# Binary cross-entropy on one core: from a software DMA queue with casting loads to one hardware queue with float32 half loads

## The chip, the core and the metric

The kernel runs on one core of a Trainium2 chip. The metric is the device time of one execution in microseconds (us). Engines: DVE is VectorE, ACT is ScalarE, POOL is GpSimd, SP is SyncE (SPq is SP's own queue of instructions). The 16 DMA engines that carry the transfers are a different thing from these engines, and they are what this study is about.

## The reference

```python
# pred, target: (8192, 8192) float32, target is 0 or 1
pred = np.clip(pred, 1e-7, 1 - 1e-7)
return -(target * np.log(pred) + (1 - target) * np.log(1 - pred))
```

Because target is 0 or 1, this equals -ln|target - 1 + clip(pred)|. Two tensors of 268 MB are read and one of 268 MB is written, with four cheap passes between.

## The kernel before

The tensors are taken as flat arrays and cut into chunks: 4096, 4096, 8192 columns, then thirty chunks of 16384, then 8192, 4096, 2048, 1024, 1024 (columns per partition, 128 partitions). A chunk is contiguous in memory, so each of the 128 partitions gets one run; in a full chunk that is 64 KiB of float32. `ring_p` holds two full chunks of pred, computed in place and stored from there. `ring_t` holds two full chunks of target in bfloat16: POOL's software queue casts while it loads.

```python
RING = 32768
SUB = 2048
ring_p = pool.tile([P, RING], fp32, ...)
ring_t = pool.tile([P, RING], bf16, ...)

def load(k):
    c, w = at(k), widths[k]
    nc.gpsimd.dma_start(out=ring_t[:, c : c + w], in_=dram(target_f, cols[k], w))
    nc.gpsimd.dma_start(out=ring_p[:, c : c + w], in_=dram(pred_f, cols[k], w))

def front(c, w):        # two DVE and two ACT instructions
    ...
def back(c, w):         # DVE: times -1
    ...
def compute(k):
    c, w = at(k), widths[k]
    n = max(1, w // SUB)
    s = w // n
    for i in range(n):
        front(c + i * s, s)
        if i:
            back(c + (i - 1) * s, s)
    back(c + (n - 1) * s, s)
```

A chunk's loads are issued as soon as the stores that free its place in `ring_p` have been issued; the pred load then waits until that store has landed, that is, until all 16 DMA engines have reported it complete.

## Time and profile before

| | |
|---|---|
| time, median of 3 runs | 1870.94 us |
| span of the profiled run | 1868.8 us |
| DVE busy, ACT busy | 63%, 52% |
| software DMA queue, share of 16 engines | 99.9% |
| HBM traffic | 805.3 MB, 431 GB/s |

These are lines of the page of the kernel before: the DMA's busy tenths, its packets, the queues with their packets, MB and share of the 16 engines' span, and the traffic.

```profile
DMA  9999999999999999999999999999999999999998
DMA packets 16427, 671.19 MB, mean 359 GB/s; under 512 B 1824, under 2 KB 1824, under 8 KB 2720
q0 software_dynamic: 16416, 671.10, 99.9%
q14 instruction: 11, 0.09, 0.0%
HBM read 536.87 MB, written 268.44 MB: 431 GB/s over the span
```

The DMA is busy all the time. 671 MB are moved as counted at the destination, because a cast target arrives as half its bytes; 805 MB is what HBM sees.

From the chain of waits (start us, length us, what), the pieces in which nothing but the transfers was waited for, every second chunk:

```profile
474.93 36.09 issue
...
591.20 36.14 issue
...
707.42 36.21 issue
```

Two chunks take 116.2 us, 58.1 us each. Now the end, by the windows view: stretch and length in us, busy us of DVE, ACT and POOL, clock, DMA share, GB/s moved.

```profile
1818.00:1832.00 14.00, 11.15 (x9) 10.27 (x6) 0.32 (x1) 1.00 1.09 435
1832.00:1845.00 13.00, 9.93 (x8) 7.53 (x4) 1.60 (x2) 1.00 0.96 416
1845.00:1853.00 8.00, 4.05 (x4) 3.82 (x2) 0.36 (x1) 1.00 0.97 420
1853.00:1858.00 5.00, 2.75 (x4) 2.11 (x2) 0.70 (x2) 1.00 0.89 378
1858.00:1861.00 3.00, 0.97 (x1) 1.97 (x2) 0.00 (x0) 1.00 0.59 242
1861.00:1863.00 2.00, 0.69 (x1) 0.15 (x1) 0.00 (x0) 1.00 0.13 55
1863.00:1865.00 2.00, 0.00 (x0) 0.00 (x0) 0.25 (x1) 1.00 0.05 20
1865.00:1867.00 2.00, 0.00 (x0) 0.00 (x0) 0.29 (x1) 1.00 0.59 242
```

The rate falls from 435 GB/s to 20 and rises once more for the last store. The timeline of the same end (start, length, engine, what, idle before it and its releaser) shows the last two instructions:

```profile
1861.18 0.69 DVE L94 TENSOR_SCALAR ring_p<-ring_p 128x1024 f32<-128x1024 f32 x1 [2.21 <-ACT ring_p L90]
1864.75 0.54 POOL L79 DMA_DIRECT2D out_dram<-ring_p  x1 [6.82 <-issue]
```

The last DVE instruction ends at 1861.87, and the last store goes out 2.9 us later: POOL hesitates once. The trace doesn't say why.

### The profile page before, as it was taken

How to read it: one execution, taken by the hardware profiler on the slowest of the kernel's cores; microseconds unless marked ns; L12 is line 12 of the kernel's file. 1: busy time of each engine (PE TensorE's matmuls, PEld its weight loads, DVE VectorE, ACT ScalarE, POOL GpSimd, SP SyncE). 2: the span in 40 equal slices, each digit the busy share in tenths (PEclk: the TensorE clock that was granted, in tenths of full speed). 3: DMA queues.
4: the chain of work that ended last, by engine and by line, in shares of the span. 5: the costliest groups of instructions: out<-in, count | busy, mean ns of one | idle time of the engine just before them, and what ended most of it. 6: DMA issues, size and time to landing. Idle time of an engine off the chain costs nothing.

```text
span 1868.8 us, 1563 instructions
## 1 busy us (share of the span) xinstructions
DVE 1178.6 (63%) x772; ACT 976.3 (52%) x516; POOL 65.4 (3%) x118
## 2 busy tenths in 40 slices
DVE  4557755577555775557755577555776556755595
ACT  3446544565444654446544466444664446644474
POOL 1000000000000000000000000000000000000010
DMA  9999999999999999999999999999999999999998
GB/s 292 359 358 338 348 400 371 337 355 342 393 386 339 341 352 387 384 351 339 345 386 389 351 344 337 383 395 344 352 344 365 400 358 339 354 355 395 374 335 349
DMA packets 16427, 671.19 MB, mean 359 GB/s; under 512 B 1824, under 2 KB 1824, under 8 KB 2720
## 3 DMA queue, kind: packets, MB, share of 16 engines
q0 software_dynamic: 16416, 671.10, 99.9%
q14 instruction: 11, 0.09, 0.0%
HBM read 536.87 MB, written 268.44 MB: 431 GB/s over the span
## 4 chain that ended last, share of the span: by engine, by line
DMA 34%; issue 30%; DVE 27%; ACT 7%; POOL 1%; another core or an unknown queue 1%; POOLq 0%; PEldq 0%
DMA ring_p<-in_pred_dram 32%; DVE ring_p L86 13%; DVE ring_p L94 7%; DVE ring_p L83 7%; ACT ring_p L89 3%; ACT ring_p L90 3%; DMA out_dram<-ring_p 2%; POOL out_dram L79 1%; POOL ring_t L74 1%; POOL ring_p L75 0%; POOLq L151 0%; POOLq L79 0%; PEldq L151 0%
## 5 line engine op out<-in xcount | busy, mean ns | idle before, releaser
L89 ACT ACTIVATE ring_p<-ring_p 128x2048 f32<-128x2048 f32 (+1 forms) x257 | 488.9, 1902 | 876.0 <-DVE ring_p L86 876.0
L83 DVE TENSOR_SCALAR ring_p<-ring_p 128x2048 f32<-128x2048 f32 (+1 forms) x257 | 312.9, 1218 | 552.9 <-DMA ring_p<-in_pred_dram 552.9
L86 DVE SCALAR_TENSOR_TENSOR ring_p<-ring_t,ring_p 128x2048 f32<-128x2048 bf16 (+1 forms) x257 | 586.9, 2284 | 8.8
L90 ACT ACTIVATE ring_p<-ring_p 128x2048 f32<-128x2048 f32 (+1 forms) x257 | 489.2, 1903 | 8.1
L94 DVE TENSOR_SCALAR ring_p<-ring_p 128x2048 f32<-128x2048 f32 (+1 forms) x257 | 313.1, 1218 | 120.8 <-ACT ring_p L90 120.8
L75 POOL DMA_DIRECT2D ring_p<-in_pred_dram x38 | 21.9, 576 | 1094.1 <-DMA out_dram<-ring_p 1084.9
L79 POOL DMA_DIRECT2D out_dram<-ring_p x38 | 22.1, 581 | 700.3 <-DVE ring_p L94 689.9
L74 POOL DMA_DIRECT2D ring_t<-in_target_dram x38 | 21.8, 574 | 5.3 <-DMA ring_t<-in_target_dram 4.4
L62 ACT ACT_TABLE_LOAD x1 | 1.3, 1283 | 0.7 <-PEq L140 0.7
L61 DVE MEMSET warm<- 1x8 f32 x1 | 0.1, 65 | 0.8 <-PEq L140 0.8
L62 ACT ACTIVATE warm<-warm 1x8 f32<-1x8 f32 x1 | 0.2, 207 | 0.0
L140 POOL MEMSET const-float32-0.0<- 128x1 f32 x1 | 0.1, 98 | 0.2 <-issue 0.2
L140 POOL MEMSET const-bfloat16-1.0<- 128x1 bf16 x1 | 0.1, 101 | 0.0
L140 POOL MEMSET const-float32-1.0<- 128x1 f32 x1 | 0.1, 98 | 0.0
L140 POOL MEMSET const-uint8-127<- 128x1 uint8 x1 | 0.1, 98 | 0.0
## 6 DMA issues: line engine op xcount, KB each, us to landing
ring_t<-in_target_dram POOLq DMA_DIRECT2D x30, 4096.0 KB, 55.6
ring_p<-in_pred_dram POOLq DMA_DIRECT2D x2, 4096.0 KB, 29.1
out_dram<-ring_p POOLq DMA_DIRECT2D x2, 4096.0 KB, 30.7
ring_p<-in_pred_dram POOLq DMA_DIRECT2D x3, 2048.0 KB, 20.9
out_dram<-ring_p POOLq DMA_DIRECT2D x3, 2048.0 KB, 53.1
ring_t<-in_target_dram POOLq DMA_DIRECT2D x2, 2048.0 KB, 37.9
ring_t<-in_target_dram POOLq DMA_DIRECT2D x3, 1024.0 KB, 16.5
ring_p<-in_pred_dram POOLq DMA_DIRECT2D x1, 1024.0 KB, 30.7
```

Source lines behind the costliest of these rows:

```text
L61: nc.vector.memset(warm, 1.0)
L62: nc.scalar.activation(out=warm, in_=warm, func=Act.Ln)
L74: nc.gpsimd.dma_start(out=ring_t[:, c : c + w], in_=dram(target_f, cols[k], w))
L75: nc.gpsimd.dma_start(out=ring_p[:, c : c + w], in_=dram(pred_f, cols[k], w))
L79: nc.gpsimd.dma_start(out=dram(out_f, cols[k], w), in_=ring_p[:, c : c + w])
L83: nc.vector.tensor_scalar(out=p, in0=p, scalar1=EPS, scalar2=1 - EPS, op0=Alu.max, op1=Alu.min)
L86: nc.vector.scalar_tensor_tensor(out=p, in0=t, scalar=1.0, in1=p, op0=Alu.subtract, op1=Alu.add)
L89: nc.scalar.activation(out=p, in_=p, func=Act.Abs)
L90: nc.scalar.activation(out=p, in_=p, func=Act.Ln)
L94: nc.vector.tensor_scalar(out=p, in0=p, scalar1=-1.0, scalar2=None, op0=Alu.mult)
L140: nc = _bacc.Bacc("TRN2", target_bir_lowering=False, num_devices=1)
```

## The change

All transfers go to SyncE's hardware queue, in an order fixed at build time. Nothing is cast on the way any more: target stays float32 and takes twice the room, so its ring is cut to half its length in columns (one full chunk), loaded in two halves of 8192 columns (32 KiB runs). Pred and out keep 64 KiB runs. A piece is what one compute instruction works on, 2048 columns here. In the last 16384 columns the final DVE pass of a piece is put off until after the first passes of the next piece, across chunks. The diff, cut to its core:

```diff
-RING = 32768
+RING_P = 32768
+RING_T = 16384
+HALF = 8192
-    ring_t = pool.tile([P, RING], bf16, name="ring_t", tag="ring_t")
+    ring_t = pool.tile([P, RING_T], fp32, name="ring_t", tag="ring_t")
...
+    def load_t(j):                       # part j: half of a full chunk
+        k, off, w = parts[j]
+        c = (cols[k] + off) % RING_T
+        rows = dram(target_f, cols[k], widths[k])
+        nc.sync.dma_start(out=ring_t[:, c : c + w], in_=rows[:, off : off + w])
+    def load_p(k): ...                   # nc.sync.dma_start, whole chunk
+    def store(k): ...                    # nc.sync.dma_start, whole chunk
...
+    queue = []
+    stored = 0
+    for k in range(len(widths)):
+        while cols[stored] + RING_P < cols[k] + widths[k]:
+            queue.append(("o", stored))
+            stored += 1
+        queue.append(("t", first_part[k]))
+        queue.append(("p", k))
+        queue += [("t", j) for j in range(first_part[k] + 1, first_part[k + 1])]
+    queue += [("o", k) for k in range(stored, len(widths))]
...
+    def compute_part():
+        ...
+        n = max(1, w // SUB)
+        for i in range(n):
+            front(...); backs.append(...)
+            while len(backs) > 1:
+                back(*backs[0]); finished = sum(backs.pop(0))
+        fronts += 1
+        chunk_done = fronts == first_part[k + 1]
+        if chunk_done and (cols[k] + w <= total - RING_T or fronts == len(parts)):
+            while backs: ...             # finish here, except in the tail
```

So a full chunk's transfers stand in the queue as: store of chunk k-2, first target half of k, pred of k, second target half of k.

More of the change, by code (lines that the diff above doesn't have):

```diff
@@ L42 @@
     fp32 = mybir.dt.float32
-    bf16 = mybir.dt.bfloat16
     Alu = mybir.AluOpType
@@ L57, with load_p, front @@
     pool = ctx.enter_context(tc.tile_pool(name="rings", bufs=1))
-    ring_p = pool.tile([P, RING], fp32, name="ring_p", tag="ring_p")
-    ring_t = pool.tile([P, RING], bf16, name="ring_t", tag="ring_t")
+    ring_p = pool.tile([P, RING_P], fp32, name="ring_p", tag="ring_p")
+    ring_t = pool.tile([P, RING_T], fp32, name="ring_t", tag="ring_t")
     warm = pool.tile([1, 8], fp32, name="warm", tag="warm")
-    nc.vector.memset(warm, 1.0)
-    nc.scalar.activation(out=warm, in_=warm, func=Act.Ln)
     widths = chunk_widths(total)
     cols = [sum(widths[:k]) for k in range(len(widths))]
-    def at(k):
-        c = cols[k] % RING
-        assert c + widths[k] <= RING
-        return c
-    def load(k):
-        c, w = at(k), widths[k]
-        nc.gpsimd.dma_start(out=ring_t[:, c : c + w], in_=dram(target_f, cols[k], w))
-        nc.gpsimd.dma_start(out=ring_p[:, c : c + w], in_=dram(pred_f, cols[k], w))
-    def store(k):
-        c, w = at(k), widths[k]
-        nc.gpsimd.dma_start(out=dram(out_f, cols[k], w), in_=ring_p[:, c : c + w])
-    def front(c, w):
-        p, t = ring_p[:, c : c + w], ring_t[:, c : c + w]
+    parts = []
+    first_part = []
+    for k, w in enumerate(widths):
+        first_part.append(len(parts))
+        n = max(1, w // HALF)
+        parts += [(k, i * (w // n), w // n) for i in range(n)]
+    first_part.append(len(parts))
+    def load_t(j):
[3 more added lines that the diff above has]
+        nc.sync.dma_start(out=ring_t[:, c : c + w], in_=rows[:, off : off + w])
+    def load_p(k):
+        c, w = cols[k] % RING_P, widths[k]
+        nc.sync.dma_start(out=ring_p[:, c : c + w], in_=dram(pred_f, cols[k], w))
+    def store(k):
+        c, w = cols[k] % RING_P, widths[k]
+        nc.sync.dma_start(out=dram(out_f, cols[k], w), in_=ring_p[:, c : c + w])
+    def front(col, w):
+        c, ct = col % RING_P, col % RING_T
+        p, t = ring_p[:, c : c + w], ring_t[:, ct : ct + w]
         nc.vector.tensor_scalar(
@@ L90, in front, with back @@
         nc.scalar.activation(out=p, in_=p, func=Act.Ln)
-    def back(c, w):
+    def back(col, w):
+        c = col % RING_P
         p = ring_p[:, c : c + w]
@@ L96, in back, with read_up_to @@
         )
-    def compute(k):
-        c, w = at(k), widths[k]
+    queue = []
[8 more added lines that the diff above has]
+    queue += [("o", k) for k in range(stored, len(widths))]
+    def read_up_to():
+        if not fronts:
+            return 0
+        k, off, w = parts[fronts - 1]
+        return cols[k] + off + w
@@ L100, in compute @@
+    fronts = 0
+    backs = []
+    finished = 0
+    def compute_part():
+        nonlocal fronts, finished
+        k, off, w = parts[fronts]
         n = max(1, w // SUB)
-        s = w // n
         for i in range(n):
-            front(c + i * s, s)
-            if i:
-                back(c + (i - 1) * s, s)
-        back(c + (n - 1) * s, s)
-    with tc.manual_schedule():
-        stored = loaded = 0
-        for k in range(len(widths)):
-            while loaded < len(widths):
-                end = cols[loaded] + widths[loaded]
-                while stored < k and end > cols[stored] + RING:
-                    store(stored)
-                    stored += 1
-                if end > cols[stored] + RING:
-                    break
-                load(loaded)
-                loaded += 1
-            compute(k)
-        while stored < len(widths):
-            store(stored)
-            stored += 1
+            col = cols[k] + off + i * (w // n)
+            front(col, w // n)
+            backs.append((col, w // n))
+            while len(backs) > 1:
+                back(*backs[0])
+                finished = sum(backs.pop(0))
+        fronts += 1
+        chunk_done = fronts == first_part[k + 1]
+        if chunk_done and (cols[k] + w <= total - RING_T or fronts == len(parts)):
+            while backs:
+                back(*backs[0])
+                finished = sum(backs.pop(0))
@@ new lines @@
+    with tc.manual_schedule():
+        for what, i in queue:
+            if what == "t":
+                k, off, w = parts[i]
+                while read_up_to() < cols[k] + off + w - RING_T:
+                    compute_part()
+                load_t(i)
+            elif what == "p":
+                load_p(i)
+            else:
+                while finished < cols[i] + widths[i]:
+                    compute_part()
+                store(i)
+            if (what, i) == ("p", 0):
+                nc.vector.memset(warm, 1.0)
+                nc.scalar.activation(out=warm, in_=warm, func=Act.Ln)
```

## The prediction

> **What bounds the kernel now.** The DMA engines. The page's queue table gives the one software queue 99.9% of 16 engines' span, while DVE is busy 63% and ACT 52%. The page counts 536.87 MB read and 268.44 MB written, 805.3 MB, 431 GB/s over the 1868.8 us span. In the middle, the chain of waits repeats every 116.2 us for two 16384-column chunks (issue pieces at 474.93, 591.20, 707.42): 58.1 us per chunk of 25.17 MB, 433 GB/s. A target load and a pred load together take 38.3 us there (store landing to pred landing), the store the other 19.8 us, so about 19.4 us per 8.39 MB transfer whatever it is; no penalty of the casting load is to be seen. The Trainium skill, "DMA: Bandwidth & Descriptors", section Specifications, puts the fabric ceiling at 435 GB/s; the trace agrees to 0.5%. So in steady state at most 0.3 us a chunk, about 9 us in all, can be won (an estimate from that figure).
>
> **What is lost outside.** By the windows view, the DMA moves 435 GB/s until 1832 us, then 416, 420, 378, 242, 55, 20 and 131 GB/s in windows up to 1868.8. That is 12.1 MB in 36.8 us, worth 27.9 us at 433: 9 us lost. There the timeline shows each store issued just after its chunk's last DVE L94, the small chunks computed one after another. About 2 us of the 9 are landing time that no order removes.
>
> **What the change does.** All transfers go from POOL to the SyncE queue; target arrives uncast (HBM bytes unchanged; SBUF writes double for it, but the reads set the time already). DVE L86 gets a float32 operand; I expect its 2.29 us unchanged. Same 64 KiB runs for pred and out, 32 KiB pieces for target.
>
> Laying transfers end to end with the durations above (19.4, target halves 9.7, 4.6 us of DVE per 2048 columns): order store(k-2), t(k) first half, p(k), t(k) second half. p(k) waits for store(k-2) landing, covered by the half target of 9.7 us behind it (before: 19.4 us): about 8 us to spare. The first half of the next target waits until the previous first half is read, 18.4 us after its pred landed, behind which lie a half target and a store (29 us): about 10 us to spare. The second half has about 20 us. So no gap, with less slack than before. In the tail, chunk 32 starts computing before store 31 rather than beside it, all loads are queued first, and the last stores find their columns finished: the tail's stores should stream at full rate, saving about 7 us of the 9. An earlier start may give 0.5 us.
>
> **Predicted:** 1870.9 - 7 - 0.5 = 1863.4; some chance that the hardware queue adds a few us through a rate nearer 435, so I say 1862 us, with 1852 to 1874 at 8 in 10. Faster by over 2%: 0.03; within 2%: 0.93; slower by over 2%: 0.04.
>
> **What would show it.** Right: windows in the middle still 58 us a chunk, moved GB/s now about 433 (no cast), DMA above 95% in the last 30 us until 3 us before the end, DVE and ACT busy times within 1%. Wrong: slices under 425 GB/s in the middle; SyncE waits on DVE with the DMA share falling beside them (ring too short); L86 longer than 2.29 us.
>
> **What would make it wrong.** A hardware queue that moves these runs at another rate than the software queue (each 1% is 19 us); a DMA engine lagging the other 15, so that landing waits eat the 8 us of slack.

## More of the kernel before

All runs were at a granted clock of 1.0.

The line of queue 14 looks like a trifle (11 packets, 0.09 MB, the fetch of the engines' own instructions).

## The result, and the profile after

Measured: 1871.85 us median (1871.53 to 1872.73, 4 runs), beside 1871.07 for the kernel before (4 runs). The ratio is 1.0005, with a 95% interval of 0.9988 to 1.0023. A ratio here is the mean time of one kernel's fast runs over that of the other's of the same rounds, so it isn't quite the ratio of the medians. The time lies in the predicted range and the class "within 2%" is right, but the gain of 7.5 to 9 us that the prediction argued for isn't there. That is a failed prediction, and that the time still lies in the range is owed to the range's width.

From the page of the changed kernel, the lines that answer to those of before:

```profile
DMA  9999999999999999999999999999999999999998
DMA packets 20749, 805.42 MB, mean 430 GB/s; under 512 B 2304, under 2 KB 2304, under 8 KB 3072
q1 hardware_dynamic: 20736, 805.32, 99.8%
q14 instruction: 13, 0.11, 0.0%
HBM read 536.87 MB, written 268.44 MB: 430 GB/s over the span
```

There are 4320 more packets in the data queue (a packet is one record of a DMA engine: a run of data, or the 4 bytes with which it reports a transfer complete). The target operand did DVE no harm: these are the group lines of that instruction in the kernel before and after, with its mean of 2284 ns in both.

```profile
L86 DVE SCALAR_TENSOR_TENSOR ring_p<-ring_t,ring_p 128x2048 f32<-128x2048 bf16 (+1 forms) x257 | 586.9, 2284 | 8.8
```

```profile
L95 DVE SCALAR_TENSOR_TENSOR ring_p<-ring_t,ring_p 128x2048 f32<-128x2048 f32 (+1 forms) x257 | 587.0, 2284 | 8.8
```

Now the end of the changed kernel by the windows view:

```profile
1832.00:1845.00 13.00, 12.43 (x10) 11.04 (x6) 0.00 (x0) 1.00 0.94 406
1845.00:1853.00 8.00, 4.35 (x5) 4.54 (x5) 0.00 (x0) 1.00 0.96 414
1853.00:1858.00 5.00, 0.00 (x0) 0.00 (x0) 0.00 (x0) 1.00 0.98 418
1858.00:1861.00 3.00, 0.00 (x0) 0.00 (x0) 0.00 (x0) 1.00 0.95 401
1861.00:1863.00 2.00, 0.00 (x0) 0.00 (x0) 0.00 (x0) 1.00 0.93 385
1863.00:1865.00 2.00, 0.00 (x0) 0.00 (x0) 0.00 (x0) 1.00 0.27 111
1865.00:1867.00 2.00, 0.00 (x0) 0.00 (x0) 0.00 (x0) 1.00 0.13 53
1867.00:1869.00 2.00, 0.00 (x0) 0.00 (x0) 0.00 (x0) 1.00 0.06 23
```

The tail does what was promised: compute is over before 1853 and the stores stream on without it until 1863. Then most of the 16 DMA engines are done, and for another 7 us four, two and at last one of them (111, 53, 23 GB/s at 27 each) finish what they still have (at the last store these four report 1.1, 1.8, 3.8 and 6.6 us after the median engine). Nothing is waited for in that time but the slowest DMA engine.

The trace has, for each transfer, the moment at which each of the 16 DMA engines reported it complete. From these I took, per full chunk, the time from one chunk's landing to the next on the median engine, and the lag: how much later than the median engine the last one reported. In the kernel before, chunks take 57.96 us once the first few are over; in the changed one 58.05. The lag grows in both, from 0.3 us at the first transfer to about 6:

```
the changed kernel, 28 chunks from about 130 us on: us a chunk (lag in us at its start)
the first eight  58.13 (0.6)  58.12 (1.2)  58.09 (1.7)  58.05 (2.1)  58.07 (2.3)  58.05 (2.5)  58.06 (3.5)  58.29 (3.5)
...
the last seven   58.06 (6.0)  58.04 (6.0)  58.12 (6.1)  58.15 (6.0)  58.74 (6.7)  58.39 (6.3)  58.06 (5.9)
the last store: median engine done at T, the one before the last at T + 3.8, the last at T + 6.6
```

And the lag grows in steps that fall on the packets of queue 14. Of the changed kernel's 13 instruction packets, six come where the last engine falls back:

```
instruction packet at about us:    427    718    968    1260   1551   1833
lag before it -> after it, us:   2.5->3.5  3.4->4.4  4.4->5.2  5.2->6.0  6.0->6.8  5.9->6.6
```

The Trainium skill, "Runtime: NRT & Kernel Launch", section "Instruction fetch mechanics", says that each engine's sequencer drives its own DMA queue to fetch its instructions while it runs. This trace agrees as far as it goes: the packets (8192 bytes, about 0.3 us each) stand in a queue of their own, and a step of the lag is 0.7 to 1.0 us. Why a packet of 0.3 us costs that much, the trace doesn't say. Of the other packets those at 581, 602, 1068, 1475 and 1633 us come where, in the order of the reports, one of the engines next to the last falls back, by 0.4 to 0.6 us.

**Theory.** One DMA engine, which carries part of the instruction fetch (the trace doesn't name it) beside its 1/16 of the data, ends up 6 us behind the others. A kernel that keeps all engines busy ends when that one ends. Before, the gaps of the tail let it catch up, so closing the gaps is worth little. The body, besides, became 0.09 us a chunk slower, 2.7 us over thirty chunks. And a pred load waits for a store's *last* engine, while the others live on what is queued behind the store, the cover: half a target, 9.7 us. When the pred load goes out, 9.0 us of it are left on the median engine at first, and 2.9 to 3.7 us once the lag is about 6. By the theory the other engines then run short of work before the load reaches them, which I call starving, and four chunks of 58.12 to 58.74 us stand there. How they lose the time is argued, not shown: the first load of the trace needs 1.0 us from issue to first data, less than the cover left; a chunk of 58.29 us comes with a lag of 3.5; and e9 below has lags up to 6.6 without such chunks.

These chunks must not be counted at the end of the kernel. The *last* engine has 9.5 to 9.7 us of cover left whenever a pred load goes out, and its own chunks from 450 us on take 58.04 to 58.13 us but for steps of 0.8 to 1.0 at the packets and one chunk of 58.33. The starved chunks slow the engines that are ahead and so shrink the lag (6.7 to 5.9 us); they hardly move the end.

**Rivals.** All engines share the tail's loss, and 7 us were really gained but given back by a slower hardware queue. Or the lag belongs to the DMA engine's place, whatever is fetched.

### The profile page after: what moved, and what is told of

It is laid out like the page before. It is cut to its first block, busy times and chain, and to the rows that moved or that the text cites. A ratio compares the mean times of both kernels' runs of the same rounds, so it can differ in the third digit from the quotient of the medians.

```text
span 1871.0 us, 1683 instructions
## 1 busy us (share of the span) xinstructions
DVE 1178.4 (63%) x772; ACT 976.3 (52%) x516; POOL 0.2 (0%) x4
## 4 chain that ended last, share of the span: by engine, by line
DMA 63%; DVE 28%; ACT 7%; issue 1%; SPq 0%
DMA out_dram<-ring_p 38%; DMA ring_p<-in_pred_dram 25%; DVE ring_p L95 13%; DVE ring_p L92 7%; DVE ring_p L104 7%; ACT ring_p L99 4%; ACT ring_p L98 4%; SPq L79 0%
## 5 line engine op out<-in xcount | busy, mean ns | idle before, releaser
L95 DVE SCALAR_TENSOR_TENSOR ring_p<-ring_t,ring_p 128x2048 f32<-128x2048 f32 (+1 forms) x257 | 587.0, 2284 | 8.8
```

The lines of the kernel that those rows point to most:

```text
L95: nc.vector.scalar_tensor_tensor(out=p, in0=t, scalar=1.0, in1=p, op0=Alu.subtract, op1=Alu.add)
```

## The experiments

All gave correct results. Times are medians of 5 runs (of 4 in e3). They ran in three batches, in each of which the kernel before ran 9 times alongside: 1870.35 us in the batch of e1 to e4, 1870.72 in that of e5 to e8, 1870.93 in that of e9 and e10. Every ratio is to the kernel before of the same batch. The changed kernel was not run again in these batches; it was 0.8 us slower than its own kernel before, and the batches' kernels before differ by 0.7 us, so differences to it are good to about 1 us at best.

### e1: the order and the tail alone

```diff
 # against the changed kernel
-RING_T = 16384
-HALF = 8192
+RING_T = 32768
+HALF = 16384
-    ring_t = pool.tile([P, RING_T], fp32, ...)
+    ring_t = pool.tile([P, RING_T], bf16, ...)
-        nc.sync.dma_start(...)        # three places
+        nc.gpsimd.dma_start(...)
```

> The new order and the pipelined tail, but on the software queue with the casting whole-chunk target loads of before. Theory (one DMA engine lags about 6 us behind the others at the end, so the tail's gaps of before were mostly filled by the laggard and only about 2 us are to be had; the body of the changed kernel is slower by about 0.1 us a chunk because of more packets): 1868.5 to 1869.5 us, a lag of about 6 us between the engines at the end, body 57.96 us a chunk. Rival (my prediction: the tail costs 7 us and all engines share it): about 1864 us.

Measured: 1869.58 us (1868.99 to 1870.42), ratio to before 0.9994 (0.998 to 1.0008). Chunks take 57.96 us, and the lag at the end is 6.2 us. The new order and tail are worth 0.8 us, not 7: a little less than my theory's 1 to 2, far from the rival's 6. The interval reaches from a gain of 3.7 us to a loss of 1.5: it excludes 7, but not nothing. The windows view of this kernel's end has the same shape as that of the changed kernel:

```profile
1858.00:1861.00 3.00, 0.00 (x0) 0.00 (x0) 0.00 (x0) 1.00 0.95 395
1861.00:1863.00 2.00, 0.00 (x0) 0.00 (x0) 0.00 (x0) 1.00 0.34 139
1863.00:1865.00 2.00, 0.00 (x0) 0.00 (x0) 0.00 (x0) 1.00 0.14 59
1865.00:1867.00 2.00, 0.00 (x0) 0.00 (x0) 0.00 (x0) 1.00 0.07 27
```

### e2: the changed kernel on the software queue

```diff
-        nc.sync.dma_start(...)        # three places
+        nc.gpsimd.dma_start(...)
```

> The changed kernel with its three transfers issued from GpSimd instead of SyncE and nothing else: float32 targets in halves. Theory (packets): the body's 0.1 us a chunk comes from the split and the 9 more packets per engine and chunk, not from the hardware queue: within 1 us of the changed kernel, body 58.05 us a chunk. Rival (the hardware queue itself is slower): body back at 57.96 us a chunk, 3 us faster than the changed kernel.

Measured: 1876.73 us (1875.29 to 1877.04), ratio 1.0031. As for the body, the theory holds: chunks undisturbed by a large lag take 58.05 us on either queue, so the hardware queue's rate is not at fault. The time is a miss, though, 5 us above the changed kernel rather than within 1. Its chunks show where part of that lies: four, entered with a lag of 4.3 to 6.0 us, take 58.18, 58.26, 60.15 and 59.31 us, together 3.7 us over 58.05. The lag alone is not the cause: before the chunk of 60.15 us POOL's one hesitation fell on the pred load, which went out 2.9 us after the store's last report (0.2 to 0.6 us in the others) with 0.4 us of cover left on the median engine. The chunk after it loses its time in the second target half (10.9 us against 9.7), on the last engine too; why, the trace doesn't say.

### e3: targets in quarters

```diff
-HALF = 8192
+HALF = 4096
```

> The changed kernel with the target loaded in quarters (16 KiB runs): 16 more data packets per engine and chunk and two more completions. Theory (packets, from start-to-start distances of 2414.5 ns for 64 KiB and 1209.5 ns for 32 KiB, so about 4.5 ns a packet, and some 20 ns for a completion and the change of size): 0.08 to 0.13 us a chunk more, 2.5 to 4 us in all, about 1875 us. Rival (queue, or waits for landings): no change, or tens of us if the ring runs dry.

Measured: 1895.27 us (1892.6 to 1897.58), ratio 1.0131: 23 us lost instead of 4. This experiment was built badly. It splits more, but it also leaves just a quarter of the target (4.8 us) between the store and the pred load that waits for it. Two stretches of the windows view, early and late:

```profile
471.00:529.00 58.00, 36.80 (x24) 30.46 (x16) 0.00 (x0) 1.00 1.01 432
1000.00:1058.00 58.00, 36.80 (x24) 30.46 (x16) 0.00 (x0) 1.00 1.00 415
```

Early the rate is near that of the changed kernel (432 GB/s); later it is 415, although the DMA share stays at 1.00: the records show packets that take longer (16 KiB up to 2.2 us, median 0.61), not engines that stand idle. The waits of SP's queue (who waited for what: us in total, times, longest) for the pred load are 823.7 us,

```profile
SPq L83 <- DMA out_dram<-ring_p: 823.7, 31, 28.5
```

against this in the changed kernel:

```profile
SPq L83 <- DMA out_dram<-ring_p: 363.4, 30, 12.9
```

These sums are not a loss by themselves: with only a quarter ahead of it SP comes to the pred load earlier and so waits longer. A chunk takes 58.2 to 58.5 us in the first eight, and mostly 59 to 60.3 later; the lag at a pred load's landing stays below 2.6 us, as if the engines ahead could no longer run away from the last one. When the pred load goes out, 1.7 to 3.2 us of cover are left on the median engine in the last fourteen chunks. That fits the starving, but e7 had to separate it from the packets.

### e4: fewer instructions

```diff
 SUB = 2048
+BODY_SUB = 8192
...
-        n = max(1, w // SUB)
+        n = max(1, w // (BODY_SUB if widths[k] == 16384 else SUB))
```

> The changed kernel with compute instructions of 8192 columns in the thirty full chunks (2048 before) and nothing changed in its transfers: a third of the DVE and ACT instructions. Theory (the laggard is the DMA engine that also carries the fetch of DVE's instructions, 0.5 to 1 us each time): instruction packets fall from 13 to about 6, the last engine lags about 2 to 3 us instead of 6.5, time down by 3 to 4 us, to about 1868. Rival (the engine is slow by its place): lag stays 6 us and the time unchanged within 0.7 us. If larger compute pieces leave the ring dry: slower by more.

Measured: 1868.13 us (1867.53 to 1868.36), ratio 0.9986 (0.9973 to 0.9998). The page has 6 instruction packets:

```profile
q14 instruction: 6, 0.05, 0.0%
```

The lag stops at 3.0 us and is 2.9 at the end; chunks take 58.06 us and none takes more in the second half. No transfer was touched, the undisturbed chunk takes what it took, and the kernel is 3.7 us faster than the changed one by the medians, 3.0 us when each is set against the kernel before of its own batch. The rival of a slow place falls as far as half of the lag is concerned.

### e5: split, or float32?

```diff
 # against e1
-HALF = 16384
+HALF = 8192
```

> The kernel of e1 (software queue, casting target loads, new order and tail) with each full chunk's target loaded in two halves. e1 ran 57.96 us a chunk in the undisturbed body, the changed kernel 58.05. If the split (8 more data packets and one completion per engine and chunk) makes the difference: 58.02 to 58.05 us a chunk, 1.5 to 2.5 us slower than e1. If float32 in place of the cast makes it: 57.97 to 57.99, within 0.7 us of e1.

Measured: 1872.24 us (1871.65 to 1873.43), 2.7 us above e1's median of the other batch; undisturbed chunks take 58.00 us. Of the 0.09 us a chunk between before and after, the split makes 0.04 (e1 to e5), and float32 in place of the cast, with the shorter ring that it needs, 0.05 (e5 to e2). Neither of my two expectations is right alone; the body's part of e5's loss is 1.2 us (0.04 times thirty), and I didn't trace the rest.

### e6: more instructions

```diff
 # BODY_SUB of e4
-BODY_SUB = 8192
+BODY_SUB = 1024
```

> The dose the other way: the changed kernel with compute instructions of 1024 columns in the full chunks, twice as many. Theory (each instruction fetch holds one DMA engine up, and the wait of the pred load for a store's last engine starves the others once the lag passes about 6 us): instruction packets 13 to about 24, the lag reaches 6 us by about the middle and stays at 6 to 7, from there on the chunks take over 58.2 us instead of 58.05; 1875 to 1878 us. Rival (the lag is a property of the engine, not of the fetches): lag and time as in the changed kernel, 1872.

Measured: 1877.51 us (1877.03 to 1880.48), ratio 1.0039, with 22 instruction packets:

```profile
q14 instruction: 22, 0.18, 0.0%
```

Chunks take 58.05 us until the lag reaches 7.0 (at the sixteenth of the 28 chunks that I followed), and from there 58.05 to 59.2, mostly over 58.2, with the lag held between 5.7 and 7.0. The expectation came true in its numbers. What delays the end, though, is the packets rather than the starving: on the last engine twelve chunks take 0.8 to 1.1 us more than 58.05, each with a packet in it (in the changed kernel five do, and its packet at 1833 us adds a sixth step). With e4 it makes a dose and its answer: 6, 13 and 22 instruction packets, 1868.1, 1871.9 and 1877.5 us, that is -2.2, +0.8 and +6.8 us against the kernel before of each batch.

### e7: quarters with the old cover

```diff
 # against e3
-        queue.append(("t", first_part[k]))
+        lead = min(first_part[k] + 2, first_part[k + 1])
+        queue += [("t", j) for j in range(first_part[k], lead)]
         queue.append(("p", k))
-        queue += [("t", j) for j in range(first_part[k] + 1, first_part[k + 1])]
+        queue += [("t", j) for j in range(lead, first_part[k + 1])]
```

> e3 again (target in quarters) but two quarters are queued before the pred load, so that as many bytes lie behind the store as in the changed kernel. Theory (e3's 23 us were starved engines, because 4.8 us of cover were less than the lag plus the issue latency; the packets alone cost 0.1 us a chunk): 58.13 to 58.2 us a chunk while the lag is under 6 us, about 1874 to 1877 us. Rival (16 KiB packets are themselves dear): about 1895 us as e3.

Measured: 1875.71 us (1875.57 to 1877.27), ratio 1.0027; 58.20 us a chunk, in the second half of the kernel within 0.02 of it in every chunk, with the lag rising to 5.5. The same packets as in e3 at the same sizes, and 20 us less: e3's loss came with the missing cover. Of the 1.3 us a chunk by which e3 is slower over the last fourteen chunks (median engine), 0.5 us lie in the pred load, as the starving has it, and 0.8 us in the last target quarter, which waits for no landing; how the one leads to the other stays open. What the packets cost is 0.15 us a chunk for 16 more data packets and two more completions per engine.

### e8: the version that the findings point to

```diff
 # e1 with BODY_SUB = 8192 of e4
```

> The version the findings point to: e1 (software queue, casting whole-chunk targets, new order and tail) with compute instructions of 8192 columns in the full chunks. Theory: body 57.96 us a chunk from e1, lag about 3 us at the end from e4, so about 3 us under e1 and 2.5 under e4: 1865.5 to 1867 us, below both kernels. If the gains don't add: 1868 or more.

Measured: 1867.87 us (1867.42 to 1868.09), against 1870.72 (1870.07 to 1872.45) for the kernel before in the same batch, ratio 0.9983 (0.9971 to 0.9996). Its page has 5 instruction packets:

```profile
q14 instruction: 5, 0.04, 0.0%
```

It is below both kernels and the fastest median, by a hair over e4 (too little to tell them apart), and 0.9 us above the range I had given. Chunks take 57.96 us as expected; the lag is 3.8 us at the end instead of 3. About 3 us of lag (3.1 by 325 us, with no instruction packet between the start and 323 us) arise early from something other than the fetch. e4 has that too: 2.7 us by about 490, with one packet, at 262 us, before that. That part of the lag stays open.

### e9: the changed kernel without its pipelined tail

```diff
-        if chunk_done and (cols[k] + w <= total - RING_T or fronts == len(parts)):
+        if chunk_done:
```

> The changed kernel with its tail pipelining taken out: every chunk finishes its last piece before the next begins, as before; transfers and their order unchanged. Theory (the end is set by the lagging DMA engine, which has work until then either way): within 1 us of the changed kernel, 1871.5 to 1873. Rival (pipelining the tail saves several us): 4 to 7 us slower.

Measured: 1872.02 us (1871.48 to 1872.23), 0.2 us from the changed kernel. The pipelining of the tail, by itself, moves nothing that can be read, as the theory says. The profiled run has no starved chunk (58.04 to 58.09 us where the lag is 5.8 to 6.6) and yet isn't clearly faster than the changed kernel, which speaks against counting those chunks at the end.

### e10: fewer instructions in the kernel before

```diff
-        n = max(1, w // SUB)
+        n = max(1, w // (BODY_SUB if w == 16384 else SUB))   # 8192
```

> The kernel before with compute instructions of 8192 columns in its full chunks, nothing else. Theory: fewer instruction fetches, the lag falls from 6 to about 4 us, but the end of this kernel is set by its late tail stores, so only part arrives: 1868.5 to 1870 us, between before and e8 (1867.87); the new order and tail are then worth 1 to 2 us beside it. Rival (the lag alone sets the end): the same time as e8.

Measured: 1873.99 us (1873.65 to 1875.3), ratio 1.0017. A clear miss: slower by 3 us instead of faster by 1 to 2. The lag did fall (3.4 us), and chunks take 57.96 us. But the larger pieces finish the last full chunk later, and every tail chunk queues behind it on DVE. From the timeline:

```profile
1864.31 0.69 DVE L95 TENSOR_SCALAR ring_p<-ring_p 128x1024 f32<-128x1024 f32 x1 [2.21 <-ACT ring_p L91]
1867.88 0.54 POOL L80 DMA_DIRECT2D out_dram<-ring_p  x1 [6.81 <-issue]
```

The last DVE instruction starts 3.1 us later than before (1864.31 to 1861.18), and so does the last store (1867.88 to 1864.75); that is the 3 us. So the end of the *before* kernel is set by its compute tail, with the lagging DMA engine close behind: it finished the store before the last 2.6 us before the very end. With the lag small, the new order and tail are worth 6.1 us beside the larger pieces (e10 to e8), of which 3 are what the larger pieces did to the old tail. A gain in the tail can only be had as far as the laggard lets it.

## Why the prediction was right or wrong

- **"What bounds the kernel now": right.** The DMA is busy throughout, and pieces of 1024, 2048 or 8192 columns leave an undisturbed chunk at 58.05 us (e6, the changed kernel, e4).
- **"The tail's stores should stream at full rate, saving about 7 us of the 9": the step that failed, in its size.** The stores do stream, but the saving measured 0.8 us (before to e1, with an interval that excludes 7 and includes 0) and 0.2 us for the pipelining alone (e9). I read the windows of before as 16 engines at a low rate. 55 and 20 GB/s are two engines and one, which still had work queued. In the kernel before the last engine was done with the store before the last only 2.6 us before the end, and in the changed one it ends 6.6 us after the median engine: the term should have been bounded by it.
- **A term was missing: the body's packets.** I wrote "at most 0.3 us a chunk, about 9 us in all, can be won" and costed the split and the loss of the cast at nothing. They cost 0.09 us a chunk, 2.7 us in all (e1, e5, e2).
- **"p(k) waits for store(k-2) landing ... about 8 us to spare": half right.** There was no dry queue in the chunks with a small lag. But the cover has to pay for the lag first, which I named only under "what would make it wrong". Of the cover, 9.0 us were left at first and 2.9 to 3.7 late. In the changed kernel four chunks lost 1.2 us there (58.12, 58.15, 58.74 and 58.39 against 58.05) on the median engine, but hardly any of it on the last, which sets the end; with less cover (e3 against e7) the whole kernel loses 20 us.
- **"A hardware queue that moves these runs at another rate": no.** e2 and the changed kernel both take 58.05 us a chunk where nothing starves.
- **L86, "I expect its 2.29 us unchanged": right**, 2284 ns in both (1024-column instructions included). **"DVE and ACT busy times within 1%": right** (1178.6 and 1178.4 us, 976.3 in both).

So the change wins 0.8 us by its order and tail and pays 2.7 us for its packets: a loss of about 1.9 us, in which the 2.7 comes from single profiled runs. Measured is 2.2 us by the two profiled spans and 0.8 us by the medians; the difference between these is below what I can separate.

## What to carry to other kernels

When all of a kernel's time is DMA, its end can be, as here, the end of the slowest of the 16 DMA engines: divide the GB/s of the last microseconds by one engine's rate before you call them a gap to close. Unrolled compute had a cost on this saturated DMA (22 instruction packets against 6: 9 us), by all that e4 and e6 show because its instructions are fetched over the same engines; larger pieces in the body, small ones only where the tail's latency counts, gave the best kernel here. A load that waits for a store to land needs cover queued behind that store, and the lag of the last engine comes off that cover before the load goes out (e3 against e7).

## What the Trainium skill lacked or had wrong

- "Runtime: NRT & Kernel Launch", "Instruction fetch mechanics", calls the cost of fetching the next block one DMA tail-bump, "mostly hidden". Whether it is hidden from the engine that fetches, no run here tests; but here a packet of 8 KiB set one data-carrying DMA engine back by 0.7 to 1.0 us, and 6, 13 and 22 of them went with 1868.1, 1871.9 and 1877.5 us. The page doesn't name this side.
- "DMA: Bandwidth & Descriptors", "Latency and other measured facts", says that some DMA engines are usually slower, with a best guess that is specific to the software queue. Here the last engine was 6.6 us behind on the hardware queue, and 5.8 (before) and 6.2 (e1) on the software queue. Which engine it is, the trace doesn't say.
- The same page, "Issuing engine by pattern", calls the hardware queue generally faster. With the same transfers, undisturbed chunks took 58.05 us on both; the whole kernel was 5 us slower on the software queue (e2), some of it in four slow chunks, one of them behind POOL's hesitation of 2.9 us.
- No page that I read says that the lag of the slowest DMA engine adds up over a kernel, here to 6 us, and that queued work has to cover it where a load waits for a store's landing (e3 against e7: 20 us).
- No page that I read gives the cost of splitting transfers at this size: 16 KiB runs in place of 32 KiB cost 0.15 us in 58 (e7 against the changed kernel), 32 KiB in place of 64 KiB 0.04 us (e1 to e5).
